# A 1024x1024 product as seven half-size products, and the order of tokens that goes with it

## The chip, the cores and the metric

The kernel runs on one core of a Trainium2 chip. The metric is the device time of one execution in microseconds. The kernel before takes 1306.87 us, the median of 3 runs (1304.11 to 1307.63). One execution of it was profiled, and its span from the first to the last instruction is 1304.7 us.

The names of the engines in the profile are PE (matrix products; PEld is its weight load), DVE and ACT (elementwise work), POOL (little elementwise work here) and SP (which only issues transfers here; the rows "SPq" are its queue).

## The reference

One layer of a hybrid network on 512 tokens of width 1024, in float32. A conditioning vector gives nine rows of modulation (`mod`), and three sublayers add to x:

```
mod = silu(c) @ w_ada + b_ada            # sh1, sc1, g1, sh2, sc2, g2, sh3, sc3, g3
u = rms_norm(x, ffn1_norm_g) * (1 + sc1) + sh1
x = x + 0.5 * g1 * swiglu(u, ffn1_w_in, ffn1_w_out)          # width 2816

u = rms_norm(x, mix_norm_g) * (1 + sc2) + sh2
z = u @ w_mix + b_mix                                        # q, k, v, gates of two branches
y_a = ... mLSTM in chunks of 64 ...;  y_b = ... forgetting attention, 16 heads ...
merged = sigmoid(g_a) * (y_a @ w_branch_a) + sigmoid(g_b) * (y_b @ w_branch_b)
x = x + g2 * (merged @ w_out)                                # 512x1024 @ 1024x1024

u = rms_norm(x, ffn2_norm_g) * (1 + sc3) + sh3
x = x + 0.5 * g3 * swiglu(u, ffn2_w_in, ffn2_w_out)
```

The change concerns the line with `w_out` and what stands around it: the branch products ahead of it, the norm and the first products of the second FFN behind it.

## The kernel before

**Products.** A 1024-deep product is cut into 8 blocks of 128 (`k`). Each float32 operand is held as two parts, high and low, and each matmul of the algorithm is three on PE (`mm3`, L139 to L143): high by high (L141), then one with a low part (L142), then the other (L143). The operand that is loaded into the array stands on the left of the comma in a profile row's inputs, the one that streams stands right. `split` makes the parts of a weight that a transfer has brought into a tile `raw`: ACT copies it into `wh` (L116), DVE subtracts into `wl` (L118). There are 3 buffers for `raw` and 4 each for `wh` and `wl`. Two groups of four accumulation banks exist, `g` and `t`. All weights come over SP's queue (L106).

**Branch stage** (`run`, L1670 to L1693). Eight products of branch a, which are called A0 to A7 here, then eight of branch b, B0 to B7. Each is 24 matmuls of 128x512 into one `g` bank, for 128 columns of the output and all 512 tokens (`branch`, L1416). Half way through a product the weights of the next are asked for. Each ends with the out step of DVE at L1430, (gate + 1) times the bank, which gives `ta` in branch a and `sg` in branch b. In branch b POOL adds the two branches' results (L1691), ACT takes the high part of the sum (`mh`, L1692) and DVE the low part (`ml`, L1693): that is `merged`, transposed, 128 columns to a tile. After each product `step` runs what is due of a chain of small work (`tick`) and one load of 512 KB of w_ada, which DVE accumulates into the modulation rows (L318, L320).

**The product with w_out** comes in two halves of its 1024 output columns. The first (`token_gemm`, L673) has a `t` bank for each block of 128 tokens; the weights come in four chunks of 256 rows, the first two for all blocks of tokens, the last two block by block, so that a finished block goes on at once: DVE scales the bank by a broadcast row (L796) and adds it to x (L798), ACT squares x with a sum (L243). The second half is in `passage` (L697), in `g` banks, block by block, and what follows is written out in a fixed order there (`pin`): the norm of the first 256 tokens (`xnorm`: the factor by a chain of small DVE instructions, L261 and L160 to L168, then `xn` at L267 on DVE and L268 on ACT), its transposes on PE (`norm_turn`, L294), the parts of u (`u_part`: L277, L279 on ACT, L283 on DVE), the same for the other 256 tokens, and the first four column groups of the second FFN's product (`first`, L771), 256 tokens at a time. `mod_cols` (L385) turns the modulation rows of the last norm into columns by a transpose on PE (L389) of what `mod_load` has fetched (L382) after a row was stored (L376).

**Order.** A scheduler places the instructions of an engine where they are not pinned, by its own costs; each engine then runs its instructions strictly in that order. The profile's rows name tiles without their numbers; the order lists give the numbers.

## Time and profile before

| | |
|---|---|
| time, median of 3 (lowest, highest) | 1306.87 us (1304.11, 1307.63) |
| span of the profiled execution | 1304.7 us |
| branch a, A0 to A7 with its last preparations | 819 to 863 us of the span |
| branch b, B0 to B7 | 863 to 906 us |
| w_out, norm, the first column groups of FFN2 | 906 to 978 us |
| PE busy | 1291.3 us |
| DVE, ACT, POOL busy | 961.2, 632.3, 34.6 us |

The profiled execution's own time is its span of 1304.7 us; what lies outside it is the 2.2 us up to the median of the runs. The page gives busy time of each engine, its share of the span, and the chain of work that ended last. A timeline row gives the start in the span, the duration, the engine, the line, the operation with output and inputs, and in brackets the idle time of that engine before it and what ended that. A window row gives, for a stretch of the span, the sum of busy time and for PE, PEld, DVE, ACT and POOL the busy time with the count of instructions, then the granted clock of PE, the share of the transfer engines, and GB/s.

### The profile page before, as it was taken

The numbers are of one execution on the slowest core, as the hardware profiler recorded it, in microseconds if no ns is written. First come the engines' busy times: TensorE is split into PE (matmuls) and PEld (weight loads), VectorE is DVE, ScalarE is ACT, GpSimd is POOL, SyncE is SP. The second block draws the span as 40 slices with busy tenths as digits, with TensorE's granted clock in tenths as the row PEclk, the third lists the DMA queues.
The fourth block names the chain that finished last, engine by engine and source line by source line (L and its number), as shares of the span: only waits on it lengthen the run. The fifth ranks groups of instructions, "written<-read, shape, count | busy, mean of one in ns | idle before, by whom it ended". The sixth has DMA issues, their size and how long they took to land.

```text
span 1304.7 us, 17739 instructions
## 1 busy us (share of the span) xinstructions
PE 1291.3 (99%) x6265; PEld 1085.2 (83%) x6265; DVE 961.2 (74%) x1740; ACT 632.3 (48%) x1040; POOL 34.6 (3%) x57
## 2 busy tenths in 40 slices
PE   8999999999999999999999999999999999999998
PEld 6788888888889888788888888888898888888887
DVE  6877777478789787999998776677566656635787
ACT  5633232355467655666574766234372223223741
POOL 1000000000010101000000000003000000000000
PEclk9999999999999999999999999999999999999999
DMA  9999978464865534545455583777539778634573
GB/s 294 276 328 303 316 266 292 139 185 155 296 187 144 173 89 130 178 133 155 138 128 149 130 151 102 230 256 242 186 114 321 257 233 278 219 97 136 167 272 143
DMA packets 245257, 260.48 MB, mean 200 GB/s; under 512 B 57312, under 2 KB 184960, under 8 KB 245168
## 3 DMA queue, kind: packets, MB, share of 16 engines
q1 hardware_dynamic: 240464, 251.41, 63.0%
q10 hardware_dynamic: 4384, 7.88, 2.0%
q8 instruction: 49, 0.80, 0.3%
q14 instruction: 40, 0.33, 0.1%
q0 software_dynamic: 320, 0.06, 0.0%
HBM read 220.43 MB, written 38.87 MB: 199 GB/s over the span
## 4 chain that ended last, share of the span: by engine, by line
PE 93%; DVE 4%; DMA 1%; ACT 1%; issue 1%; POOL 0%; ACTq 0%; DVEq 0%; POOLq 0%; SPq 0%
PE g L142 24%; PE g L141 24%; PE g L143 24%; PE t L141 4%; PE t L142 4%; PE t L143 4%; PE g L949 2%; PE t L1362 1%; PE t L1332 1%; PE t L1305 1%; PE t L949 1%; PE t L1306 1%; PE t L837 0%; DVE wl L118 0%; DMA h_d<-hn 0%
## 5 line engine op out<-in xcount | busy, mean ns | idle before, releaser
L116 ACT ACTIVATE wh<-raw 128x1024 fp32r<-128x1024 f32 (+2 forms) x246 | 248.9, 1016 | 348.8 <-PE g L142 109.9
L118 DVE TENSOR_TENSOR wl<-raw,wh 128x1024 fp32r<-128x1024 f32 (+2 forms) x246 | 288.1, 1175 | 155.0 <-ACT wh L116 131.0
L141 PE MATMUL g<-uh,wh 128*128 128x512 f32 (+1 forms) x880 | 340.9, 387 | 0.0
L143 PE MATMUL g<-uh,wl 128*128 128x512 f32 (+1 forms) x880 | 339.6, 386 | 0.0
L142 PE MATMUL g<-ul,wh 128*128 128x512 f32 (+1 forms) x880 | 339.1, 385 | 0.0
L143 PEld LDWEIGHTS g<-uh,wl 128*128 128x128 f32 x880 | 165.3, 188 | 33.6
L141 PEld LDWEIGHTS g<-uh,wh 128*128 128x128 f32 x880 | 165.4, 188 | 32.9 <-issue 0.6
L142 PEld LDWEIGHTS g<-ul,wh 128*128 128x128 f32 x880 | 165.4, 188 | 32.2
L141 PE MATMUL g<-wh,uh 128*128 128x512 f32 (+1 forms) x256 | 97.6, 381 | 0.0
L143 PE MATMUL g<-wh,ul 128*128 128x512 f32 (+1 forms) x256 | 96.6, 377 | 0.0
L142 PE MATMUL g<-wl,uh 128*128 128x512 f32 (+1 forms) x256 | 96.5, 377 | 0.0
L320 DVE SCALAR_TENSOR_TENSOR acc<-raw,ccol,acc 128x1024 f32<-128x1024 f32 (+1 forms) x56 | 56.7, 1032 | 40.1 <-DMA raw<-in_w_ada_dram 40.0
L141 PE MATMUL t<-wh,A 128*128 128x512 f32 x176 | 68.6, 390 | 0.0
L142 PE MATMUL t<-wl,A 128*128 128x512 f32 x176 | 68.6, 390 | 0.0
L143 PEld LDWEIGHTS g<-wh,ul 128*128 128x128 f32 x256 | 48.2, 188 | 8.9
L142 PEld LDWEIGHTS g<-wl,uh 128*128 128x128 f32 x256 | 48.3, 188 | 8.4
L141 PEld LDWEIGHTS g<-wh,uh 128*128 128x128 f32 x256 | 48.2, 188 | 8.2
L141 PE MATMUL g<-yh,wh 128*128 128x512 f32 x128 | 49.8, 389 | 0.0
L143 PE MATMUL g<-yh,wl 128*128 128x512 f32 x128 | 49.8, 389 | 0.0
L142 PE MATMUL g<-yl,wh 128*128 128x512 f32 x128 | 49.8, 389 | 0.0
L1316 ACT ACTIVATE S<-S,mn 128x128 f32<-128x128 f32 (+1 forms) x64 | 35.6, 557 | 26.2 <-DVE mn L1308 20.4
L460 ACT ACTIVATE A<-E 128x768 fp32r<-128x768 f32 x22 | 18.6, 846 | 52.6 <-DVE E L459 52.6
(370 smaller groups left out, 2230.3 us busy)
## 6 DMA issues: line engine op xcount, KB each, us to landing
raw<-in_ffn_w_in_dram SPq DMA_DIRECT2D x82, 512.0 KB, 4.9
raw<-in_w_ada_dram SPq DMA_DIRECT2D x48, 512.0 KB, 4.8
raw<-in_w_mix_dram SPq DMA_DIRECT2D x46, 512.0 KB, 4.3
sa<-in_ffn_w_out_dram SPq DMA_DIRECT2D x22, 512.0 KB, 5.4
sb<-in_ffn_w_out_dram SPq DMA_DIRECT2D x44, 256.0 KB, 5.7
ws<-sa SPq DMA_DIRECT2D x22, 512.0 KB, 4.8
ws<-sb SPq DMA_DIRECT2D x44, 256.0 KB, 3.8
raw<-ws SPq DMA_DIRECT2D x44, 256.0 KB, 3.6
```

The costliest lines, as they stand in the source:

```text
L116: nc.scalar.activation(hi, src, AF.Copy)
L118: self.last_lo = nc.vector.tensor_tensor(lo, src, hi, op=SUB)
L141: pin(mm(ps, lh, rh, start=start, stop=False))
L142: pin(mm(ps, lh, rl, start=False, stop=False))
L143: self.last_mm = pin(mm(ps, ll, rh, start=False, stop=stop))
L320: nc.vector.scalar_tensor_tensor(a, r[:, s], c, a, op0=MUL, op1=ADD)
L460: nc.scalar.activation(A1[:, 0:3, :], E[:, 0:3, :], AF.Copy)
L949: pin(nc.tensor.matmul(acc_ps[b], (wl if p == 1 else wh)[:, b % 2, s], self.ul[k] if p == 2 else self.uh[k], start=k == 0 and p == 0, stop ...
L1305: nc.tensor.matmul(ps[:, :w], q[:, s], k[:, :w], start=True, stop=False)
L1306: nc.tensor.matmul(ps[:, :w], q[:, s], kl[:, :w], start=False, stop=True)
L1316: nc.scalar.activation(S[:, ws], S[:, ws], AF.Exp, scale=-1.0, bias=m, accum_out=sm[:, qb:qb + 1])
L1332: tr = lambda b, c, qb, kb: nc.tensor.transpose(b[:, c:c + P], S[:, P_OFF[qb] + kb * P:P_OFF[qb] + (kb + 1) * P], self.ident)
```

## The change

**Seven products in place of eight.** With the 1024 columns of `merged` cut into even and odd blocks of 128 (A1 and A2, so E and Ra in the code) and the 512 tokens into the first and last 256, and w_out cut into even and odd row blocks and into two halves of its columns, the product is a 2x2 product of blocks, done by seven block products with sums on both sides (the form of Strassen's scheme with few additions). Each block product is 256 tokens by 512 rows by 512 columns: two banks, 24 matmuls of 128x512. Seven make 168 matmuls, where the kernel before has 192.

**Sums of weights** (`out_sums`). During branch a, after each product, one step of a generator loads a pair of row blocks of w_out (four transfers of 256 KB into tiles that u has left free), makes four sums by DVE subtractions (L689 to L692), held behind the low part of the weights that was made last, and stores them (four transfers of 256 KB) to scratch memory. Four pairs make 32 transfers.

**Sums of merged** (`merge_slot`, `merge_pair`). POOL's add writes into `mt`, which uses the tiles of x. After each second product of branch b, DVE and ACT make the seven left operands of that pair in high and low parts: eight DVE instructions of 128x256 or 128x512 and four of ACT. They take the place of L1692 and L1693. x is loaded later, behind the merges.

**The passage** is written anew. The products run in the order A11, A12, S2, S1, S4, S3, A22. A11, S2, S1 and S4 go one onto the other in the same two `t` banks; ACT copies the banks out after each of the first three (`p1`, `u2`, `u4`). A12 is in two `g` banks, S3 and A22 one onto the other in two more. `into` scales a result and adds it to x (L777, L779, L780). Tokens 0 to 255 are complete after S4: their norm runs then, and their transposes stand on PE behind S3. Tokens 256 to 511 are complete after A22. Parts, `first` and the second norm follow.

```diff
-    def mm3(self, ps, lh, ll, rh, rl, start, stop):
+    def mm3(self, ps, lh, ll, rh, rl, start, stop, on=False):
...
+    def out_sums(self, w):
+        nc = self.nc
+        V = nc.vector.tensor_tensor
+        self.wo = [self.dp.tile([P, NK // 2, 512], F32, name=self.nm("wo")) for _ in range(4)]
+        tags = [f"{a}{k}" for k in range(NK) for a in ("uh", "ul")]
+        ts = {}
+        def load(i):
+            ts[i] = [self.up.tile([P, 512], F32, name=self.nm("so"), tag=tags[5 * (i % 3) + n]) for n in range(5)]
+            with self.tc.issue_after(self.last_raw.ins):
+                for n, (r, h) in enumerate(((0, 0), (0, 1), (1, 0), (1, 1))):
+                    nc.sync.dma_start(ts[i][n], w[(2 * i + r) * P:(2 * i + r + 1) * P, h * 512:(h + 1) * 512])
+        def sums(i):
+            a, b, c, d, e = ts[i]
+            with self.tc.issue_after(self.last_lo.ins):
+                V(e, d, b, op=SUB)
+                V(b, b, a, op=SUB)
+                V(d, d, b, op=SUB)
+                V(c, c, d, op=SUB)
+        def store(i):
+            a, b, c, d, e = ts.pop(i)
+            for t, o in zip((b, e, c, d), self.wo):
+                nc.sync.dma_start(o[:, i, :], t)
...
+    def merge_pair(self, i, bp):
+        E, Ra, S, Rb = self.mt
...
+        nc.scalar.activation(A[:, 0, :], E[:, 0, :], AF.Copy)
+        V(A[:, 1, :], E[:, 0, :], A[:, 0, :], op=SUB)
+        nc.scalar.activation(Rah, Ra, AF.Copy)
+        V(Ral, Ra, Rah, op=SUB)
+        V(S[:, 0, :], E[:, 1, :], Ra[:, 1, :], op=ADD)
+        V(S[:, 1, :], S[:, 0, :], E[:, 0, :], op=SUB)
+        nc.scalar.activation(Sh, S, AF.Copy)
+        V(Sl, S, Sh, op=SUB)
+        V(Rb[:, 1, :], Ra[:, 0, :], S[:, 1, :], op=SUB)
+        V(Rb[:, 0, :], E[:, 0, :], E[:, 1, :], op=SUB)
+        nc.scalar.activation(Rbh, Rb, AF.Copy)
+        V(Rbl, Rb, Rbh, op=SUB)
...
-    def passage(self, lhs, w_out, w_in, bp, G, sh):
+    def passage(self, w_out, w_in, bp, gain):
...
+        weights("A11")
+        weights("A12")
...
+        for tb in range(2):
+            product("A11", Z, tb, True)
+            pin(nc.scalar.activation(p1[tb], Z[tb], AF.Copy))
...
+        weights("S2")
+        X = [self.gbank() for _ in range(2)]
+        product("A12", X, 0, True)
+        product("A12", X, 1, True)
...
+        t = into(0, 0, X[0], p1[0])
+        product("S2", Z, 0)
...
+        weights("S4")
+        product("S1", Z, 0)
...
+        m3 = self.mod_load(6)
+        weights("S3")
+        apart(2)
+        product("S4", Z, 0)
+        t = into(0, 1, Z[0])
+        self.x_sq(0, 1, t)
+        product("S4", Z, 1)
+        G, sh3 = self.mod_cols(6, gain, m3, self.tbank)
+        t = into(1, 1, Z[1])
+        self.x_sq(1, 1, t)
+        weights("A22")
+        V4 = [self.gbank() for _ in range(2)]
         xn = self.xnorm(0, bp)
...
+        product("S3", V4, 0, True)
...
         b = self.norm_turn(0, xn)
...
+        for tb in range(2):
+            product("A22", V4, tb)
+        for k in range(NK):
+            part(0, k)
...
             for m in range(NK):
                 ta.append(self.branch(m, 0, bp, yp.tile([P, T], F32, name=self.nm("ta"), tag="qk", bufs=16), sg[m] if m < 2 else None))
                 step()
+                next(pw, None)
...
-                nc.gpsimd.tensor_tensor(t, t, ta[m], op=ADD)
-                nc.scalar.activation(self.mh[m], t, AF.Copy)
-                nc.vector.tensor_tensor(self.ml[m], t, self.mh[m], op=SUB)
+                nc.gpsimd.tensor_tensor(self.merge_slot(m), t, ta[m], op=ADD)
+                if m % 2:
+                    self.merge_pair(m // 2, bp)
```

**What moves.** Three places on DVE. The first is branch a. `ta_8251`, `ta_8288` and `ta_8327` are the out steps of A1, A2 and A3 before, `wl_8346`, `wl_8385`, `wl_8424` and `wl_8463` the low parts of the weights of A4 to A7:

```order
L1430 SCALAR_TENSOR_TENSOR ta_8251<-sg_8101,g_8252 128x512
L118 TENSOR_TENSOR wl_8346<-raw_8343,wh_8345 128x1024
L320 SCALAR_TENSOR_TENSOR acc_8134<-raw_8362,ccol,acc_8134 128x512
L320 SCALAR_TENSOR_TENSOR acc_8135<-raw_8362,ccol,acc_8135 128x512
L118 TENSOR_TENSOR wl_8385<-raw_8382,wh_8384 128x1024
L1430 SCALAR_TENSOR_TENSOR ta_8288<-sg_8289,g_8291 128x512
```

In the changed kernel `ta_8298`, `ta_8354` and `ta_8410` are the out steps of A2, A3 and A4, `wl_8373` and `wl_8429` the low parts of A4 and A5:

```order
L1531 SCALAR_TENSOR_TENSOR ta_8298<-sg_8299,g_8301 128x512
L1531 SCALAR_TENSOR_TENSOR ta_8354<-sg_8355,g_8357 128x512
L118 TENSOR_TENSOR wl_8373<-raw_8370,wh_8372 128x1024
L320 SCALAR_TENSOR_TENSOR acc_8118<-raw_8389,ccol,acc_8118 128x512
L320 SCALAR_TENSOR_TENSOR acc_8119<-raw_8389,ccol,acc_8119 128x512
L689 TENSOR_TENSOR so_8345<-so_8344,so_8342 128x512
L690 TENSOR_TENSOR so_8342<-so_8342,so_8341 128x512
L691 TENSOR_TENSOR so_8344<-so_8344,so_8342 128x512
L692 TENSOR_TENSOR so_8343<-so_8343,so_8344 128x512
L1531 SCALAR_TENSOR_TENSOR ta_8410<-sg_8411,g_8413 128x512
L118 TENSOR_TENSOR wl_8429<-raw_8426,wh_8428 128x1024
```

Before, the low part of A4 stood ahead of the out step of A2; now it stands behind the out step of A3, the product just ahead of A4, and the same holds for A5 (behind A4), A6 and A7. On PE, A4 follows A3 so; its third matmul reads `wl_8373`:

```order
L143 MATMUL g_8357<-yh_8188,wl_8317 128x512
L141 MATMUL g_8413<-yh_8160,wh_8372 128x512
L142 MATMUL g_8413<-yl_8161,wh_8372 128x512
L143 MATMUL g_8413<-yh_8160,wl_8373 128x512
```

The first of these rows is A3's last matmul, and the others are A4's first three.

The second place is the end of branch b. Before, `sg_8861` is the out step of the last but one product, and the weights of the first w_out chunks follow with one low part of `merged` between them:

```order
L1430 SCALAR_TENSOR_TENSOR sg_8861<-sg_8861,g_8863 128x512
L118 TENSOR_TENSOR wl_8988<-raw_8985,wh_8987 128x1024
L1693 TENSOR_TENSOR ml_8099<-sg_8861,mh_8091 128x512
L118 TENSOR_TENSOR wl_8994<-raw_8991,wh_8993 128x1024
```

After, `sg_8976` is the out step of B7, `mt_8973` and `mt_8974` with `mr` and `mo` belong to the last pair's merge, `wl_9048` and `wl_9054` are the two halves of A12's weights:

```order
L1531 SCALAR_TENSOR_TENSOR sg_8976<-sg_8976,g_8978 128x512
L765 TENSOR_TENSOR wl_9048<-raw_9045,wh_9047 128x1024
L730 TENSOR_TENSOR mt_8973<-mt_8971,mt_8972 128x256
L729 TENSOR_TENSOR mr_9014<-mt_8972,mr_9013 128x512
L731 TENSOR_TENSOR mt_8973<-mt_8973,mt_8971 128x256
L734 TENSOR_TENSOR mt_8974<-mt_8972,mt_8973 128x256
L733 TENSOR_TENSOR mo_9012<-mt_8973,mo_9011 128x512
L737 TENSOR_TENSOR mr_9016<-mt_8974,mr_9015 128x512
L765 TENSOR_TENSOR wl_9054<-raw_9051,wh_9053 128x1024
```

The second half of A12's weights now stands behind the whole merge of the last pair, which cannot begin before B7 has ended.

The third place is the first norm. Before, the last rows ahead of its chain (L261, L160 and so on) are the low parts of a column group of FFN2 and one block's scale and add:

```order
L722 TENSOR_TENSOR fl_9168<-raw_9164,fh_9166 128x512
L722 TENSOR_TENSOR fl_9169<-raw_9164,fh_9167 128x512
L796 SCALAR_TENSOR_TENSOR rs_9196<-g_9079,gb_9076 128x512
L798 TENSOR_TENSOR x_8900<-x_8900,rs_9196 128x512
L261 SCALAR_TENSOR_TENSOR v_9218<-ss_8913 128x2
L160 TENSOR_SCALAR rq_9220<-v_9218 128x2
```

After, `t_9031` and `t_9032` are the banks after S4, and `wl_9321` and `wl_9327` the weights of A22:

```order
L793 TENSOR_TENSOR fl_9274<-raw_9270,fh_9272 128x512
L793 TENSOR_TENSOR fl_9275<-raw_9270,fh_9273 128x512
L779 SCALAR_TENSOR_TENSOR rs_9292<-t_9031,gb_9101 128x512
L779 SCALAR_TENSOR_TENSOR rs_9314<-t_9032,gb_9101 128x512
L780 TENSOR_TENSOR x_9058<-x_9058,rs_9292 128x512
L780 TENSOR_TENSOR x_9060<-x_9060,rs_9314 128x512
L765 TENSOR_TENSOR wl_9321<-raw_9318,wh_9320 128x1024
L765 TENSOR_TENSOR wl_9327<-raw_9324,wh_9326 128x1024
L261 SCALAR_TENSOR_TENSOR v_9332<-ss_9029 128x2
L160 TENSOR_SCALAR rq_9334<-v_9332 128x2
```

Two blocks of tokens end together now, and both halves of A22's low part stand between their adds and the chain of the norm.

More of the change, by code (lines that the diff above doesn't have):

```diff
@@ new lines, in passage, with part @@
+        b = self.norm_turn(0, xn)
+        x_spill((0, 1))
+        hi0, lo0 = whole(0)
+        hi3, lo3 = whole(3)
+        def part(hf, k):
+            self.u_part(hf, b, k, bp, G, sh3, True, V)()
+        for tb in range(2):
+            product("A22", V4, tb)
+        for k in range(NK):
+            part(0, k)
+            if k == 1:
+                hi0()
+            if k == 3:
+                lo0()
+        for tb in range(2):
+            into(tb + 2, 1, ts[tb])
+            self.x_sq(tb + 2, 1, ts[tb])
@@ L769, in passage @@
+        for tb in range(2):
+            t = into(tb + 2, 0, V4[tb])
+            self.x_sq(tb + 2, 0, t)
+        hi3()
         xn = self.xnorm(1, bp)
+        lo3()
         pp = [self.gbank() for _ in range(4)]
@@ L782, in passage @@
         for k in range(NK):
-            part(1, b, k, True)
+            part(1, k)
         first(1, (0, 1))
@@ L1670, in run @@
         with tc.tile_pool(name="br", bufs=1) as bp:
[L1671 to L1672 removed]
+            pw = self.out_sums(A["w_out"][0])
+            self.ma = {}
             def step():
```

202 lines of the change are left out of this document (102 added, 100 removed).

## The prediction

> **What bounds the kernel now.** I read the page first.
>
> ```profile
> span 1304.7 us, 17739 instructions
> PE 1291.3 (99%) x6265; PEld 1085.2 (83%) x6265; DVE 961.2 (74%) x1740; ACT 632.3 (48%) x1040; POOL 34.6 (3%) x57
> PE 93%; DVE 4%; DMA 1%; ACT 1%; issue 1%; POOL 0%; ACTq 0%; DVEq 0%; POOLq 0%; SPq 0%
> ```
>
> PE is busy 99% of the span and is 93% of the chain that ended last. So matmuls taken away are worth their full issue interval, and every wait that PE gains is paid in full. The windows of the three stages say the same of the place that changes, and how full DVE and the transfers are there:
>
> ```profile
> 819.00:863.00 44.00, 44.00 (x196) 36.44 (x195) 29.29 (x41) 15.86 (x21) 0.00 (x0) 1.00 0.79 238
> 863.00:906.00 43.00, 43.00 (x192) 35.34 (x191) 35.13 (x44) 15.51 (x20) 10.74 (x7) 1.00 0.83 270
> 906.00:978.00 72.00, 72.00 (x424) 63.43 (x423) 41.54 (x79) 39.23 (x72) 2.81 (x2) 1.00 0.48 151
> ```
>
> PE has no idle time in 159 us. DVE is busy 29.3 of 44 us in branch a, 35.1 of 43 in branch b, 41.5 of 72 behind them. Of the waits of PE, the groups of the whole span that lie here are two, together 2.1 us:
>
> ```profile
> PE t L372 <- DVE hl L367: 1.8, 1, 1.8
> PE t L294 <- DVE xn L267: 0.3, 1, 0.3
> ```
>
> The question is therefore not what an engine's total becomes, but whether the new orders make PE wait for more than the removed matmuls gave.
>
> **What is removed: 24 matmuls.** From PE's timeline across the end of A1 and the start of A2; the first and the last of these rows are eleven matmuls apart:
>
> ```profile
> 828.43 0.39 PE L141 MATMUL g<-yh,wh 128*128 128x512 f32 x1
> 829.56 0.39 PE L143 MATMUL g<-yh,wl 128*128 128x512 f32 x1
> 830.92 0.39 PE L143 MATMUL g<-yh,wl 128*128 128x512 f32 x1
> ```
>
> (830.92 − 828.43) / 11 = 0.226 us from one to the next, so 24 fewer are 5.4 us, and one block product, also 24, lasts 5.4 us. The w_out product has no stall that could swallow the gain, by the windows. **Gain 5.4.**
>
> **Term 1, branch a, four waits.** The row at 829.56 above is the last matmul of its product: DVE's out step follows it.
>
> ```profile
> 829.99 0.69 DVE L1430 SCALAR_TENSOR_TENSOR ta<-sg,g 128x512 f32<-128x512 f32 x1 [0.22 <-PE g L143]
> 833.22 1.22 DVE L118 TENSOR_TENSOR wl<-raw,wh 128x1024 fp32r<-128x1024 f32 x1 [2.54 <-ACT wh L116]
> 834.36 1.41 DVE L320 SCALAR_TENSOR_TENSOR acc<-raw,ccol,acc 128x512 f32<-128x512 f32 x2
> 857.19 0.69 DVE L1430 SCALAR_TENSOR_TENSOR ta<-sg,g 128x512 f32<-128x512 f32 x1 [1.88 <-PE g L143]
> 857.79 0.88 DVE L318 TENSOR_SCALAR acc<-raw,ccol 128x512 f32<-128x512 f32 x2
> ```
>
> Now the low part of the next product's weights stands behind the out step, for A4 to A7. With t the start of the last matmul: out step at t + 0.43 (829.99 − 829.56), the next DVE instruction 0.60 later (857.79 − 857.19), the low part takes 1.22: it is there at t + 2.25. The third matmul of the next product reads it and would start at t + 3 x 0.226 = t + 0.68. That is 1.57 us each, 6.3 for four. Nothing covers it: PE is in strict order and its next rows are of the same product. The low end is 6.0 (a low part at 1.14, its spacing to the next row, 834.36 − 833.22), the high end 6.3. This alone takes more than the gain.
>
> The sums' own work is hidden at first. Sixteen subtractions of about 0.6 us are 9.6 us in A0 to A6 on a DVE with 14.7 us free of 44. The transfers are nearer to a bound: 0.79 of 44 us is 34.8 us of busy time now, and 32 transfers of 256 KB are 8.4 MB, which at the best rates the trace shows
>
> ```profile
> 980.00:982.00 2.00, 2.00 (x11) 1.65 (x10) 0.47 (x2) 0.85 (x1) 0.00 (x0) 1.00 0.99 390
> 982.00:984.00 2.00, 2.00 (x11) 1.65 (x10) 1.50 (x3) 0.99 (x1) 0.00 (x0) 1.00 1.01 404
> ```
>
> take 21 us. Less four loads of x that now come later (1 MB, 2.6 us), that is 53 us of transfers in 44 + 6.3 = 50.3 us. Weights arrive ahead of their use: the low part made at 833.22 is for A4, and A2 starts with the matmul behind the row at 829.56, so A4 two products later, at 840.6. So 3 us can be late without a wait. I take 0, with 3 as the high end.
>
> **Term 2, branch b.** POOL's add gates each merge, and its duration swings:
>
> ```profile
> 882.76 1.29 POOL L1691 TENSOR_TENSOR sg<-sg,ta 128x512 f32<-128x512 f32 x1 [4.95 <-DVE sg L1430]
> 900.27 2.14 POOL L1691 TENSOR_TENSOR sg<-sg,ta 128x512 f32<-128x512 f32 x1 [3.57 <-DVE sg L1430]
> ```
>
> The low part of B3's weights now stands behind the first pair's merge, which waits for the add behind B1's out step. The operations of half width cost about 0.34 by this row and the next one, which starts 0.34 later:
>
> ```profile
> 978.57 0.42 DVE L458 TENSOR_TENSOR E<-E,Ra 128x256 f32<-128x256 f32 x1
> 978.91 1.22 DVE L118 TENSOR_TENSOR wl<-raw,wh 128x1024 fp32r<-128x1024 f32 x1
> ```
>
> Chain from B1's last matmul: 0.43 + 0.60 + add 2.14 + 0.34 + 0.34 + 0.60 + 0.34 + 0.60 + 0.60 + 1.22 = 7.2 us. B2 with three matmuls of B3 is 27 x 0.226 = 6.1. So 1.1, or 0.25 with the short add. I take 1.0; range 0.2 to 1.8, the top with other merges that meet a full DVE (35.1 us of 43, and eight instructions, 5 x 0.34 + 3 x 0.60 = 3.5 us, come for two of 0.60 in each pair).
>
> *The shared port.* The Trainium skill, "SBUF — State Buffer", section "Who interferes with whom", says that a VectorE operation with two inputs in SBUF and a GpSimd operation that reads SBUF exclude one another for the whole instruction. The two rows above, 1.29 and 2.14 for the same add, fit it; by that rule the merges, all of two SBUF inputs, would push the adds towards the long one, and term 2 goes to its 1.1.
>
> **Term 3, the second half of A12's weights.** It stands behind the last pair's merge. From B7's last matmul at t8, by the same prices: the add ends at 0.43 + 0.60 + 2.14 = 3.17, ACT's copy of 0.63 behind it at 3.80, then DVE's 0.60 + 0.34 + 0.34 + 0.60 + 0.60 and the low part's 1.22: t8 + 7.5, and 7.7 with a wait for the second copy. Its first reader is the eighth matmul of A12, 32 after t8: t8 + 7.2. That would be 0.4 if DVE were idle at t8. It is rather full: with 2.3 us more for each pair it has 44 us of work in 43, and one pair's merge, 3.5 to 4, can still stand ahead. I take the middle, 2.5; range 0.4 to 4.5.
>
> **Term 4, the modulation columns in S4.** The row is stored and read back before the transpose on PE:
>
> ```profile
> 919.20 0.26 SPq L376 DMA_DIRECT2D mod_d<-br  x1
> 922.63 0.38 SPq L382 DMA_DIRECT2D mr<-mod_d  x1
> DMA to landing us min/median/max: 3.6/3.6/3.6
> ```
>
> 3.4 + 3.6 = 7.0 us after the row is ready, which follows two small matmuls at A12's end. The transpose stands 36 matmuls, 8.2 us, later, and SP's queue is shared with w_in's loads. Behind it the low part of S4's weights waits for two scale-and-adds: about 1.2 by the same prices. Together 1.5; range 0 to 3.
>
> **Term 5, the first norm.** Before, 24 matmuls of the last block and a lead of a whole block covered it but for the 0.3 above. Rows of the chain:
>
> ```profile
> 944.42 0.63 ACT L243 ACTIVATE rs<-x 128x512 f32<-128x512 f32 x1 [3.35 <-DVE x L798]
> 945.18 0.16 DVE L261 SCALAR_TENSOR_TENSOR v<-ss 128x2 f32<-128x2 f32 x1 [0.85 <-ACT rs L243]
> 946.76 0.88 DVE L267 TENSOR_SCALAR xn<-x,rq 128x512 f32<-128x512 f32 x2
> ```
>
> Now, from the last matmul of S4 at e: 0.43, two DVE steps 1.20, the add 0.69, the square with its sum 0.76 to the start of L261; but ACT's copies of A22's weights wait for S4's end, since their buffers are S4's, and DVE's two low parts of them (1.22 + 1.14) stand ahead of L261. A copy is 1.02 by the page:
>
> ```profile
> L116 ACT ACTIVATE wh<-raw 128x1024 fp32r<-128x1024 f32 (+2 forms) x246 | 248.9, 1016 | 348.8 <-PE g L142 109.9
> ```
>
> Sum: 0.43 + 1.20 + 0.69 + 0.76 + 1.06 (a copy with its issue) + 1.22 + 1.14 + 1.58 (946.76 − 945.18) + 0.88 = 9.0. S3 covers 24 x 0.226 = 5.4, and 0.2 of start: 3.3 to 3.6. FFN2's column group, whose low parts stand ahead of all this, has a transfer of 512 KB to wait for, 4.9 us by the page's row:
>
> ```profile
> raw<-in_ffn_w_in_dram SPq DMA_DIRECT2D x82, 512.0 KB, 4.9
> ```
>
> So I take 4.0; range 3.0 to 5.5. If L261 didn't stand behind the two low parts, it would be 1.2.
>
> **Term 6, the second norm.** A22 ends; then four scale-and-adds on DVE behind the eight low parts of u, four squares and the chain. ACT's sixteen part rows at 0.45 each
>
> ```profile
> 949.81 0.56 ACT L277 ACTIVATE uh<-t,sh,G 128x256 fp32r<-128x256 f32 x1
> 950.26 0.56 ACT L279 ACTIVATE uf<-t,sh,G 128x256 f32<-128x256 f32 x1
> 975.41 0.28 PE L141 MATMUL g<-uh,wh 128*128 128x256 f32 x1
> 975.53 0.28 PE L142 MATMUL g<-ul,wh 128*128 128x256 f32 x1
> ```
>
> with a copy of weights are 8.3, the eight DVE steps of 0.60 behind them 4.8, the last square 0.8, the chain 1.6 and xn 0.9: 16.4 us from the transposes. A22 (5.4) and 72 matmuls of 256 columns at 0.12 (975.53 − 975.41; 8.6), with the wait for the first parts, are some 15.2. Take 1.2; range 0 to 2.5.
>
> **Sum.** 6.3 + 1.0 + 2.5 + 1.5 + 4.0 + 1.2 = 16.5 lost, 5.4 gained: +11.1. On the profiled execution 1304.7 + 11.1 = 1315.8; it lies 2.2 below the median of the runs, so 1318 against 1306.87. All low ends: 6.0 + 0.2 + 0.4 + 0 + 3.0 + 0 − 5.4 = +4.2, 1311. All high ends with the transfers: 6.3 + 3 + 1.8 + 4.5 + 3 + 5.5 + 2.5 − 5.4 = +21, 1328.
>
> **The rivals.** *A, the waits don't come about.* Decides: the low parts of A4 to A7 are made early enough after all, because the out steps are not what they wait for at run time, and the passage is covered as before. The point is a wait under 5.4 / 4 = 1.36 us per product in branch a with nothing behind it. For it: PE never waited at 819 to 978 before. Against it: DVE is in strict order, and 1.57 is a sum of three rows. Time: with all six terms at nothing 1301.5, faster.
>
> *B, only branch a stalls.* While PE waits 6.3 us there, ACT, the transfers and DVE run on, and the later chains find their covers. For it: DVE is only 41.5 of 72 us busy behind the branches. Against it: terms 3 and 5 are chains from the end of a product, and no lead shortens these. Time: 1306.87 + 6.3 − 5.4 + 0.5 = 1308.
>
> *C, transfers bound branch a.* 53 us of them in 50, and if the lead is gone, A5 to A7 wait for raw weights, and DVE, which then waits for `so` tiles ahead of the out steps, holds the out steps too. Price: the 3 us over and another 4 for order. For it: 0.79 of the engines' time is in use already. Against: the lead of one product. Time: 1318 + 7 = 1325.
>
> *D, the waits are long enough to slow PE's clock.* After the first wait of the kernel, 6 us, matmuls of one size take 0.208 each, and 0.12 later:
>
> ```profile
> PE t L212 <- DMA rowsC<-in_b_ada_dram: 6.0, 1, 6.0
> ...
> 6.18 6.24 PE L837 MATMUL t<-ident 128*128 128x128 f32 x30
> 12.26 1.95 PE L853 MATMUL t<-ccol,ar 128*128 128x128 f32 x16
> ```
>
> If terms 3 and 5 are near their high ends, 4.5 and 5.5 (3.5 over the sum), and do the same, each costs up to 6.24 − 30 x 0.122 = 2.6 us more: 1318 + 3.5 + 5.2 = 1327. For it: these rows. Against it: the granted clock of the windows above is 1.00 throughout, and no row of a mid-span wait shows a slower matmul. The Trainium skill, "TensorE: Matmul & The Clock Gate", section "Part 1: The HAM clock gate", says that the clock falls to half after an idle window of about 3.4 us and comes back after as long of work. By that rule term 5 at 4.0 would pay it and term 3 at 2.5 not.
>
> That the change doesn't do what it says isn't a rival: the product rows on PE are 24 fewer.
>
> **How the numbers follow.** Forecast, the sum with its terms within their ranges: 0.62. A 0.08, B 0.15, C 0.07, D 0.08. The likeliest is the sum, 1318; its own range is 1311 to 1328. With B the range to give reaches down to 1307; A and the ends of C stay outside: 1307 to 1328. What a measurement here can tell from no change is about 0.3%, 3.9 us. Faster is A, 0.08. Within 0.3%, 1303 to 1310.8, is B without its upper part, 0.13, and a little of the forecast's low end, 0.02. Slower is the rest, 0.77.
>
> **What would show it.** In the profile after: waits of PE for `wl` at L118 (or its line in the passage), four of 1.6 us in branch a, each behind an out step of DVE; if they are absent or under 1.36, term 1 is wrong and A nearer. One wait for `wl` at L765 seven matmuls into A12 (term 3), and one at the transposes, L294, for `xn` of about 4 us (term 5). The w_out products should take 168 x 0.226 = 38 us of PE time. Waits for `wh` or `raw` in branch a would speak for C, a granted clock under 1.00 after 880 us for D. The forecast is wrong if the waits of PE behind 819 us sum to under 9 us.

## The result, and the profile after

The changed kernel takes 1338.56 us, the median of 4 runs (1334.32 to 1339.58), where the kernel before took 1305.76 beside it. The ratio is 1.0243, with an interval of 1.0223 to 1.0264: 32 us slower, outside the range of 1307 to 1328. The profiled execution's span is 1337.0 us, 32.3 over the one before, and it is that difference which is divided up here.

The page of the changed kernel, its first rows and the chain that ended last:

```profile
span 1337.0 us, 17823 instructions
PE 1298.4 (97%) x6241; PEld 1085.2 (81%) x6241; DVE 995.1 (74%) x1794; ACT 643.7 (48%) x1060; POOL 37.0 (3%) x57
PE 79%; DVE 9%; DMA 6%; ACT 2%; issue 2%; SPq 1%; POOL 0%; POOLq 0%; ACTq 0%; DVEq 0%
```

PE runs 24 fewer instructions and is busy 7 us longer, so some of its matmuls have become slower. Its share of the chain fell from 93% to 79%, and the share of transfers (DMA) rose from 1% to 6%. The waits of PE by group, those of a microsecond or more, but for the kernel's opening one. A row gives the engine and bank, the line that waited, what ended the wait, then the total in us, how often, and the longest:

```profile
PE g L143 <- DVE wl L118: 6.7, 6, 2.0
PE t L294 <- DVE xn L267: 6.2, 3, 5.3
...
PE g L141 <- ACT wh L116: 4.7, 2, 3.8
PE t L142 <- DVE wl L765: 4.5, 2, 3.5
PE g L142 <- DVE wl L765: 3.4, 1, 3.4
PE t L141 <- ACT u L840: 1.0, 1, 1.0
```

Where the stages begin and end is read from the first and last matmul with `yh`, the last out step with `ta`, and the first matmul of FFN2 that has 512 columns. Before:

```profile
L141 PE MATMUL g<-yh,wh x128: 389/389/398, 818.9 to 905.8; 128*128 128x512 f32 x128
...
L1430 DVE SCALAR_TENSOR_TENSOR ta<-sg,g x8: 677/680/690, 825.3 to 862.9; 128x512 f32<-128x512 f32 x8
...
977.57 0.40 PE L141 MATMUL g<-uh,wh 128*128 128x512 f32 x1
```

and after:

```profile
L141 PE MATMUL g<-yh,wh x128: 388/389/629, 817.7 to 922.0; 128*128 128x512 f32 x128
...
L1531 DVE SCALAR_TENSOR_TENSOR ta<-sg,g x8: 675/687/691, 824.5 to 873.6; 128x512 f32<-128x512 f32 x8
...
1009.70 0.40 PE L141 MATMUL g<-uh,wh 128*128 128x512 f32 x1
```

Branch a lasted 44.0 us and lasts 55.9; branch b, up to two matmuls (0.6 us) after the last of these `yh` rows, 43.5 and 49.0; the rest up to FFN2's full-width matmuls 71.2 and 87.1. So the loss is 11.9, 5.5 and 15.9 us, the last with the 5.4 of the removed matmuls already in it; the stage starts 1.2 earlier, and what follows is as long as before. Gross that is 38.7 us of loss against a forecast of 16.5. Windows of the changed kernel, which do not follow the stages exactly, since these now end at 873.6, 922.6 and 1009.7:

```profile
819.00:865.00 46.00, 38.73 (x159) 30.26 (x158) 28.03 (x39) 7.46 (x8) 0.00 (x0) 0.96 1.01 330
865.00:913.00 48.00, 43.85 (x182) 34.45 (x181) 40.79 (x59) 17.02 (x26) 10.05 (x5) 0.96 0.66 197
913.00:989.00 76.00, 61.69 (x273) 49.83 (x272) 57.03 (x90) 40.27 (x68) 5.50 (x4) 0.91 0.63 200
```

Three things stand in them: a transfer share of 1.01 in branch a (0.96 over its whole 55.9 us), where it had been 0.79; idle time of PE in all three; and a granted clock under 1.00 in all three, where it had been 1.00.

### The profile page after: what moved, and what is told of

It reads as the page before. It is cut to its first block, busy times and chain, and to the rows that moved or that the text cites. A ratio compares the mean times of both kernels' runs of the same rounds, so it can differ in the third digit from the quotient of the medians.

```text
span 1337.0 us, 17823 instructions
## 1 busy us (share of the span) xinstructions
PE 1298.4 (97%) x6241; PEld 1085.2 (81%) x6241; DVE 995.1 (74%) x1794; ACT 643.7 (48%) x1060; POOL 37.0 (3%) x57
## 4 chain that ended last, share of the span: by engine, by line
PE 79%; DVE 9%; DMA 6%; ACT 2%; issue 2%; SPq 1%; POOL 0%; POOLq 0%; ACTq 0%; DVEq 0%
PE g L143 20%; PE g L142 20%; PE g L141 20%; PE t L141 3%; PE t L142 3%; PE t L143 3%; PE t L1463 1%; PE g L1050 1%; PE t L1433 1%; DVE wl L118 1%; DMA raw<-in_w_branch_a_dram 1%; PE t L1406 1%; PE t L1407 1%; ACT wh L116 1%; PE t L1050 1%
## 5 line engine op out<-in xcount | busy, mean ns | idle before, releaser
L116 ACT ACTIVATE wh<-raw 128x1024 fp32r<-128x1024 f32 (+2 forms) x238 | 240.6, 1015 | 354.8 <-PE g L142 129.9
L118 DVE TENSOR_TENSOR wl<-raw,wh 128x1024 fp32r<-128x1024 f32 (+2 forms) x238 | 276.9, 1167 | 138.0 <-ACT wh L116 118.5
L142 PEld LDWEIGHTS g<-ul,wh 128*128 128x128 f32 x880 | 165.5, 188 | 32.3
```

The lines of the kernel that those rows point to most:

```text
L116: nc.scalar.activation(hi, src, AF.Copy)
L118: self.last_lo = nc.vector.tensor_tensor(lo, src, hi, op=SUB)
L142: pin(mm(ps, lh, rl, start=False, stop=False, skip_group_check=on))
```

## Branch a: order or bytes

Theory one was the forecast's: the low parts of A4 to A7 stand behind the out steps on DVE. Theory two is the rival C: the transfers of the sums fill the stage. Rows of the changed kernel from SP, ACT, PE and DVE around A5 and A6:

```profile
836.85 4.12 SPq L684 DMA_DIRECT2D so<-in_w_out_dram  x4
...
842.52 0.38 SPq L106 DMA_DIRECT2D raw<-in_w_branch_a_dram  x1
...
849.79 1.06 ACT L116 ACTIVATE wh<-raw 128x1024 fp32r<-128x1024 f32 x1 [9.28 <-DMA raw<-in_w_branch_a_dram]
...
850.90 0.50 PE L141 MATMUL g<-yh,wh 128*128 128x512 f32 x1 [3.75 <-ACT wh L116]
...
859.78 1.22 DVE L118 TENSOR_TENSOR wl<-raw,wh 128x1024 fp32r<-128x1024 f32 x1
...
861.05 0.50 PE L143 MATMUL g<-yh,wl 128*128 128x512 f32 x1 [1.52 <-DVE wl L118]
```

The wait at 861.05 is theory one's: 1.52 us idle, 1.7 from start to start, for a price of 1.57. But such a wait stands only in A6 and A7. Ahead of A5 PE waits 3.75 us for a weight tile whose transfer was issued at 842.5 and landed 7 us later, and that is theory two's. Six runs divide the two.

**Only the order put right.** In branch a the out step is held behind the next low part:

```diff
-        nc.vector.scalar_tensor_tensor(dst, sg, 1.0, ps, op0=ADD, op1=MUL)
+        with self.tc.issue_after(self.last_lo.ins) if i == 0 else nullcontext():
+            nc.vector.scalar_tensor_tensor(dst, sg, 1.0, ps, op0=ADD, op1=MUL)
```

> The changed kernel with one thing different: in branch a the out step of a product is held behind the low part of the next product's weights on DVE, so that no low part waits for an out step. Theory one (the order on DVE is what branch a loses, four waits of 1.6 us): about 6 us come back, 1332 us, and PE's waits for wl in branch a are gone. Theory two (the 32 transfers of the sums fill branch a, and the weights come late whatever the order): at most 3 us come back, 1336 to 1339 us, and PE's waits for wl turn into waits for wh behind transfers of raw.

It took 1334.95 us (ratio to before 1.0232, 1.0211 to 1.0252), an interval that overlaps the changed kernel's: by the medians 3.6 us came back, by the ratios 1.4, so that a gain isn't clear of the noise. The waits of A6 and A7 are gone; the one for `wh` stays as it was, as the groups of this run show (the row with `wl` is A4's and B3's):

```profile
PE g L141 <- ACT wh L116: 4.0, 2, 3.8
...
PE g L143 <- DVE wl L118: 2.1, 2, 1.6
```

Branch a, measured as above, still lasted 52.7 us in this run's profile, 8.7 more than before. The time lies between the two theories' forecasts; the waits that are left are theory two's.

**No sums at all.**

```diff
-               "S1": sum_w(T1), "S3": sum_w(T3), "A22": sum_w(T4), "S2": sum_w(T2)}
+               "S1": raw_w(0, 1), "S3": raw_w(0, 0), "A22": raw_w(1, 0), "S2": raw_w(1, 1)}
...
-            pw = self.out_sums(A["w_out"][0])
...
-                next(pw, None)
```

> The changed kernel without the sums of w_out: no loads, subtractions or stores in branch a, and the four block products that took a sum take a plain block of w_out (so the product with w_out isn't computed rightly). Both theories: branch a lasts 43.5 us again in place of 55.5, and the rest stays as it is, 1326 us. If the late transfers also feed the waits behind branch a, the later stages shorten too, to 1318. What stays over 1305.8 + 5.4 - 5.4 is the price of the merges and the passage alone.

1320.3 us (1.0119; 1.0099 to 1.0139). Both branches are as long as before, branch b with all its merges:

```profile
L141 PE MATMUL g<-yh,wh x128: 389/389/397, 818.5 to 905.4; 128*128 128x512 f32 x128
```

86.9 us from the first to the last of these, like the 86.9 before. So the 17.4 us of the two branches are not there without the sums of weights, and the passage alone costs 15 us more than it did. The time came out near the 1318 that stood for late transfers that carry on into the later stages.

**The sums alone, and their bytes.** Two runs put the sums into the kernel before, unused. The second makes them an eighth as wide:

```diff
-                    nc.sync.dma_start(ts[i][n], w[(2 * i + r) * P:(2 * i + r + 1) * P, h * 512:(h + 1) * 512])
+                    nc.sync.dma_start(ts[i][n][:, 0:64], w[(2 * i + r) * P:(2 * i + r + 1) * P, h * 512:h * 512 + 64])
...
-            a, b, c, d, e = ts[i]
+            a, b, c, d, e = [x[:, 0:64] for x in ts[i]]
...
-                nc.sync.dma_start(o[:, i, :], t)
+                nc.sync.dma_start(o[:, i, 0:64], t[:, 0:64])
```

> The kernel before, with the sums of w_out made and stored in branch a as in the changed kernel, and not used. It prices the sums with the old passage behind them. If branch a's loss is its own and is not made worse by what follows: 12 us over before, 1318 us. If only the order on DVE costs: 6.3, 1312 us. If the old passage takes part of it back, because its own transfers and low parts are ahead by then: less.

> The kernel before with the sums in branch a as in the run that only adds them (1316.1 us), but every one of the 32 transfers and 16 subtractions covers 64 columns in place of 512: the same count in the same places of SP's queue, an eighth of the bytes. If the bytes are what branch a loses: 1305 to 1307 us. If the places in SP's queue are (each group of four ahead of the next weights): 1312 to 1316 us. DVE's order comes out a little better here, the low part ahead of the out step for A4, A6 and A7, so up to 3 us less than 1316 say nothing on either.

The sums alone: 1316.11 us (1.0089; 1.0071 to 1.0106), 12 us over before; its branch a loses 11 us and its branch b, which has no merges of pairs, 1. Thin: 1305.46 us (1.0014; 1.0002 to 1.0025). The window of branch a, first of the sums alone, then thin:

```profile
819.00:863.00 44.00, 37.49 (x154) 29.23 (x153) 27.41 (x37) 7.51 (x8) 0.00 (x0) 0.96 0.99 337
```

```profile
819.00:863.00 44.00, 43.12 (x189) 34.96 (x188) 29.18 (x51) 14.62 (x20) 0.00 (x0) 1.00 0.79 240
```

The same 32 issues stand in SP's queue in both, and with an eighth of the bytes they cost some 3 us at most. So the bytes bind: in the first window the transfer engines are at 0.99 with 337 GB/s. The subtractions are an eighth as wide too, but the wait ahead of A5 ended on ACT's copy, which had waited for a transfer and not for DVE, and DVE was busy only 27.4 of 44 us with the full sums. In the thin run most low parts also stand ahead of the out steps, since smaller sums changed the scheduler's order, and this run alone doesn't clear the order. The next two do their part.

**The order alone, no sums.**

```diff
+                if 3 <= n < NK - 1:
+                    sh = [P, NK, P]
+                    r = self.raw(sh, [(lambda t: t, A["w_branch_a"][0][:, (n + 1) * P:(n + 2) * P].rearrange("(k p) n -> p k n", p=P))])
+                    self.w_next = [self.wp.tile(sh, F32R, name=self.nm(s), tag=s, bufs=4) for s in ("wh", "wl")]
+                    nc.scalar.activation(self.w_next[0], r, AF.Copy)
+                    self.w_late = r
...
+        if self.w_late is not None and 3 <= n < NK - 1:
+            with self.tc.issue_after(last.ins):
+                self.last_lo = nc.vector.tensor_tensor(self.w_next[1], self.w_late, self.w_next[0], op=SUB)
```

> As the run without the sums, and in branch a the low parts of A4 to A7 are put behind the out steps of A3 to A6 on DVE, as they stand in the changed kernel. It prices the order alone, with no transfer of the sums beside it. Theory one: 6.3 us over the run without the sums, four waits of PE of 1.6 us start to start. If a clock drop is behind much of branch a's loss, it would not show here, since each wait is under 2 us.

1332.1 us (1.0214; 1.0197 to 1.0231), 12 over the run without sums, where 6.3 was expected. The group of waits for `wl`, then the two matmuls of PE around the longest wait, then the SP row of the transfer that it ended on:

```profile
PE g L143 <- DVE wl L1540: 5.4, 3, 1.9
```

```profile
841.53 0.39 PE L142 MATMUL g<-yl,wh 128*128 128x512 f32 x1
844.98 0.79 PE L141 MATMUL g<-yh,wh 128*128 128x512 f32 x1 [3.06 <-ACT wh L1532]
```

```profile
840.07 0.38 SPq L106 DMA_DIRECT2D raw<-in_w_branch_a_dram  x1
```

Three waits for `wl` of 1.5 to 1.9 are the forecast's. The fourth is another: this edit also moved PE's order. The first two matmuls of A5 and of A6 now stand ahead of A4's third, as the order of PE has it (the numbers tell the tiles apart; the trace has the same lines from 840.85 to 846.00):

```
L141 MATMUL g_8353<-yh_8160,wh_8329 128x512
L142 MATMUL g_8353<-yl_8161,wh_8329 128x512
L141 MATMUL g_8392<-yh_8160,wh_8368 128x512
L142 MATMUL g_8392<-yl_8161,wh_8368 128x512
L141 MATMUL g_8431<-yh_8160,wh_8407 128x512
L142 MATMUL g_8431<-yl_8161,wh_8407 128x512
L143 MATMUL g_8353<-yh_8160,wl_8330 128x512
```

So at 844.98 PE waits in A4 for A6's weights. These were asked for at 840.07, where the run without sums asks at 835.11: there are three `raw` buffers, and one whose low part is made late comes free late. The clock is at half for 6.8 us from 844.10, near the end of that wait. The run shows that waits of the forecast's size come when a low part stands behind the out step, three where four were expected; the order's whole price it doesn't show, since the mixed rows on PE are its own and not the changed kernel's. In the changed kernel the order put right gave back 1.4 to 3.6 us; nearly all of branch a's 12 came back only where the bytes were gone.

**The sums on another queue.** The same sums in the kernel before, their transfers issued by POOL.

```diff
-                    nc.sync.dma_start(ts[i][n], w[(2 * i + r) * P:(2 * i + r + 1) * P, h * 512:(h + 1) * 512])
+                    nc.gpsimd.dma_start(ts[i][n], w[(2 * i + r) * P:(2 * i + r + 1) * P, h * 512:(h + 1) * 512])
...
-                nc.sync.dma_start(o[:, i, :], t)
+                nc.gpsimd.dma_start(o[:, i, :], t)
```

> The kernel before with the same sums at full size, their 32 transfers issued on POOL's queue in place of SP's, so that no weights stand behind them; the low parts stand well ahead of the out steps again on DVE. If the bytes bind (53 us of transfers in 44): branch a still loses most, 1313 to 1316 us, with waits for wh behind raw. If SP's queue and DVE's order bind: 1305 to 1308 us.

1321.25 us (1.0127; 1.0112 to 1.0142), 5 us more than on SP's queue. Low parts stood ahead of the out steps here, and branch a still waits 4.2 us for `wh` and, at its end, 4.5 for `yh`. That agrees with theory two. Why POOL's queue is worse than SP's was not looked into.

## Behind the branches: two places in DVE's order

The wait that the forecast did not have stands in A11. Rows of the changed kernel from PE, DVE and POOL:

```profile
929.18 0.50 PE L142 MATMUL t<-wl,mo 128*128 128x512 f32 x1 [3.52 <-DVE wl L765]
...
926.84 2.29 DVE L765 TENSOR_TENSOR wl<-raw,wh 128x1024 fp32r<-128x1024 f32 x1
...
926.47 1.58 POOL L1793 TENSOR_TENSOR mt<-sg,ta 128x512 f32<-128x512 f32 x1 [7.93 <-DVE sg L1531]
```

The second half of A11's weights is made on DVE behind the third pair's merge and B6's out step, and DVE comes there late. It also takes 2.29 us in place of 1.22: POOL's add runs from 926.47 to 928.05, and the low part ends 1.08 after it. The Trainium skill, "SBUF — State Buffer", section "Who interferes with whom", says that a DVE operation with two inputs in SBUF and a GpSimd (POOL) operation that reads SBUF exclude one another; these rows agree, though one pair of rows doesn't show it to be the cause.

The second place is the first norm. Rows of DVE and PE:

```profile
966.11 1.28 DVE L779 SCALAR_TENSOR_TENSOR rs<-t,gb 128x512 f32<-128x512 f32 x2
...
970.40 2.36 DVE L765 TENSOR_TENSOR wl<-raw,wh 128x1024 fp32r<-128x1024 f32 x2 [1.81 <-ACT wh L764]
972.67 0.15 DVE L261 SCALAR_TENSOR_TENSOR v<-ss 128x2 f32<-128x2 f32 x1
...
974.25 0.88 DVE L267 TENSOR_SCALAR xn<-x,rq 128x512 f32<-128x512 f32 x2
...
974.79 3.86 PE L294 MATMUL t<-ident,xn 128*128 128x128 f32 x16 [5.34 <-DVE xn L267]
```

The chain is as forecast, with the two low parts of A22 just ahead of L261. The next runs all leave the sums of weights out, as above, so that the passage stands alone: 1320.3 us, with waits of 4.9 in A11, 2.0 in A12 and 5.0 at the transposes. A11's:

```profile
PE t L142 <- DVE wl L763: 4.9, 1, 4.9
```

**The add on DVE.**

```diff
-                nc.gpsimd.tensor_tensor(self.merge_slot(m), t, ta[m], op=ADD)
+                nc.vector.tensor_tensor(self.merge_slot(m), t, ta[m], op=ADD)
```

> As the run without the sums (1320.3 us), and the add of the two branches ahead of each merge is on DVE in place of POOL. Theory M (DVE runs 8 to 10 us late at the end of branch b because each merge waits on a round trip over POOL, and the low parts of A11's and A12's weights are queued behind that): the waits in A11 and A12, 4.9 and 2.0 us, fall under 2 and 1 us, the slow-clock stretches after them go, and about 8 us come back: 1312 us. Theory F (DVE is simply full there): eight adds of 0.6 us more make it later, the waits stay or grow: 1320 to 1325 us.

1315.66 us (1.0075; 1.0053 to 1.0096). The wait in A11 is gone and that in A12 is 2.2:

```profile
PE g L142 <- DVE wl L763: 2.2, 1, 2.2
```

So theory M holds for the first and not for the second, and of the 8 us expected 4.6 came by the medians, 5.7 by the ratios: A12's second half stands behind the last pair's merge wherever the add is made. In its place a new wait of 1.6 came for the modulation row (`mr`, L389), which the earlier delay had covered.

**A22's low parts behind xn.** In the passage `weights("A22")` makes only the high parts, and the subtractions follow the norm.

```diff
-        weights("A22")
+        lows = weights("A22", True)
...
+        for f in lows:
+            f()
```

> As the run without the sums, and the two low parts of A22's weights stand behind the first norm's xn on DVE instead of ahead of its chain. Theory N (those two stand in the norm's way): the wait at the transposes falls from 5.0 to about 2.6 us, and the slow stretch behind it goes or shortens: 1316 to 1318 us. If the chain waits for something else (the square, ACT's copies), it stays at 5.0 and 1320 us.

1315.92 us (1.0078; 1.0058 to 1.0097); the wait at the transposes fell from 5.0 to 1.8:

```profile
PE t L294 <- DVE xn L267: 2.8, 3, 1.8
```

Theory N holds. Not all of the gain is the norm's: A12's wait fell from 2.0 to 0.9 too, though the edit doesn't touch it, and no slow stretch stood behind it, so that the transposes began 4.2 us earlier after the branches, 3.1 of them by their own wait. A new wait of 1.0 for `rs` came right behind them.

**Both of these edits together.**

> As the run without the sums, with the add on DVE and A22's low parts behind the norm, both. If the two waits are separate: the sum of the two single gains, about 1308 to 1310 us by theories M and N. If the first stage's gain lets the norm begin earlier and changes nothing in its chain, the same sum; if less, the waits share a cause.

1309.33 us (1.0035; 1.0024 to 1.0046): by the ratios 5.7 and 5.4 us alone, 11.0 together (the bare medians give 4.6, 4.4 and 11.0, but the kernel before took 1303.71 beside the run without sums and 1305.49 beside these three). The two add, so they are separate.

**The rest of the passage in order.** The last pair's sums moved behind A12's low parts, the second column group's parts behind the norm, A22's low parts behind the two adds after it.

```diff
+        with tc.issue_after(self.low_last.ins):
+            self.merge_rest()
...
-        apart(2)
+        parts2 = apart(2, True)
...
+        for f in lows:
+            f()
...
+        parts2()
         hi0, lo0 = whole(0)
```

> As the run without the sums (so the product isn't computed rightly), with the passage put in order: adds on DVE; the last pair's sums, all but its Ra parts, behind the low parts of A12; the second column group's parts of FFN2 behind the first norm and A22's low parts behind the two adds after it. Theory M and N together (each wait of the passage is a place in DVE's order, not lack of time): the waits of 2.2, 1.9 and 1.0 us that were left go, with the slow stretch, some 7 us under the run with both changes: 1302 us, faster than before. If the chains themselves are too long for five products: 1306 to 1309 us.

1315.39 us (1.0078; 1.0063 to 1.0093): 6 us worse than the run with both, where 7 better was expected. Its groups:

```profile
PE t L294 <- DVE xn L267: 2.5, 3, 1.9
PE g L143 <- DVE wl L811: 2.5, 1, 2.5
PE t L141 <- ACT u L844: 2.1, 1, 2.1
...
PE g L142 <- DVE wl L768: 0.9, 1, 0.9
```

A12's wait fell from 2.2 to 0.9, and the first norm's from 1.9 to 0.2, as meant (the 1.9 left in that row is the second norm's). But the second group's `raw` is now held until 950, the next load of FFN2 waits for its buffer (issued at 949.5, where the run with both had one at 943.3), and ACT waits 2.3 us in the middle of the parts of u: a new wait of 2.5 for that weight and 1.9 at the second norm. The 2.1 for `u`, absent in the run with both, is another: ACT's copy of a bank stands behind copies of weights that waited 3.2 and 1.1 us for transfers of w_out. The theory that each wait is only a place in an order falls here; waits removed were paid for by later loads.

**The whole change with all of it.** The last run has the sums of weights, the edit of branch a's order from the first run, and the edits of the passage just shown.

> The changed kernel, with the sums, the out steps of branch a behind the next low part, and the passage in the order of the run before this. If the parts add: 1338.6 - 3.6 - (1320.3 - what the passage alone gives, about 1302) = 1317 us. If late transfers of branch a also hold the passage back: 1320 to 1325 us.

1329.31 us (1.0192; 1.0175 to 1.0209), 9 under the changed kernel and 25 over before. That is what the single results add to: 1338.6 − 3.6 − (1320.3 − 1315.4) = 1330.1. The forecast of 1317 had the passage alone at 1302.

## The clock

**Work that keeps PE busy.** 20 matmuls that nobody reads stand in the first norm's wait.

```diff
+        fb = self.gbank()
+        for _ in range(20):
+            pin(nc.tensor.matmul(fb, self.ma["S3"][0][0][:, 0:P], ops["S3"][0][0][:, 0, :], start=True, stop=True))
         b = self.norm_turn(0, xn)
```

> As the run without the sums, and 20 matmuls that compute nothing used stand between S3 and the transposes of the first norm, 4.5 us of the 5.0 that PE waits there. Theory C (a long wait makes PE's clock run at half for a stretch behind it): no slow stretch behind that wait in the records of the clock, and from the first transpose to the first matmul of FFN2's column groups 7.4 us in place of 9.2: 1318.5 us. If the transposes are slow for another reason: no change, 1320.3 us, or a little slower if the filler delays them.

The transposes, first without the filler and then with it:

```profile
957.58 3.86 PE L294 MATMUL t<-ident,xn 128*128 128x128 f32 x16 [4.97 <-DVE xn L267]
...
966.78 0.28 PE L141 MATMUL g<-uh,wh 128*128 128x256 f32 x1
```

```profile
957.51 2.25 PE L294 MATMUL t<-ident,xn 128*128 128x128 f32 x16 [0.62 <-DVE xn L267]
...
965.08 0.28 PE L141 MATMUL g<-uh,wh 128*128 128x256 f32 x1
```

16 transposes take 2.25 us in place of 3.86, and the stretch up to FFN2's first matmul 7.6 in place of 9.2: theory C. The kernel's time stayed at 1321.27 us (1.0116; 1.0095 to 1.0136), because the second norm's wait grew from 0.5 to 1.8 us. What the clock gave back there, the next chain took.

How long a wait must be is read from windows of 3.41 us laid on the clock's own steps. Of the changed kernel:

```profile
889.99:893.40 3.41, 1.42 (x7) 0.88 (x6) 3.41 (x7) 2.21 (x3) 0.00 (x0) 1.00 0.52 152
893.40:896.82 3.42, 3.42 (x9) 2.64 (x9) 3.42 (x6) 0.00 (x0) 2.34 (x1) 0.50 0.52 153
924.12:927.53 3.41, 1.54 (x6) 0.93 (x6) 3.35 (x6) 1.61 (x3) 1.06 (x1) 1.00 0.87 280
927.53:930.95 3.42, 1.77 (x8) 1.45 (x9) 3.38 (x5) 1.36 (x2) 0.51 (x1) 1.00 0.69 205
```

In the first, PE is idle for 1.99 us, and the second runs at 0.50. The wait of 3.52 us in A11 falls on two windows, 1.87 and 1.65 idle, and no slow one follows. Over the profiles of all runs with slow stretches, 30 such windows had 1.94 us or more without work on PE, four of them already at half clock, and a slow one followed each. At full clock three more had 1.89 to 1.93, followed by a slow one twice, and after 1.88 or less none was slow. Behind a slow window the next was slow too where it had 0.52 us or more without work, and not where it had 0.36 or less. A slow stretch of the changed kernel is 3.4 or 6.8 us long, and there are four. From 939.0 matmuls start 0.43 apart:

```profile
938.40 0.80 PE L142 MATMUL g<-wl,mr 128*128 128x512 f32 x1 [3.45 <-DVE wl L765]
939.00 0.63 PE L143 MATMUL g<-wh,mr 128*128 128x512 f32 x1
939.42 0.63 PE L141 MATMUL g<-wh,mr 128*128 128x512 f32 x1
```

Half of what PE worked in the four is 1.7 + 1.7 + 3.1 + 2.0 = 8.5 us.

## Why the prediction was wrong

The direction and the gain were right, the size was not: +32 where +11 was forecast. Of the gross loss of 38.7 us in the profiled run, 26 are idle time of PE in 14 waits, 8.5 the slow clock, and the rest, 4, is the 0.3 us that each wait costs beyond its idle time (0.16 up to the slot that the matmul ahead leaves, and a first interval of 0.34 in place of 0.23). One reading of the profile before was wrong as well, and no term rests on it: the two waits that the prediction puts in these stages, 2.1 us together, stood at 530.8 and 387.2 us, so there PE had no wait at all.

- **Term 1 (6.3; measured 11.9).** The step that failed is its second half: "3 us can be late without a wait. I take 0". The lead of two products was read from the kernel before, in an order where weights are asked for early. In the changed kernel SP's queue has the sums' groups ahead of them, and it stands still while earlier transfers land: of the 4.12 us of the four loads at 836.85 each is issued in 0.33 to 0.45, and the rest are gaps of up to 1.4. The 53 us of transfers in 50 that the term worked out were right (0.96 of 55.9 is 53.7), and that left no lead. Idle time is 8.7 of the 11.9, half a slow stretch 1.7, the rest what each wait costs beyond it. The thin run shows that the bytes decide. The order's own price was right for each wait (1.52 and 1.46 idle), and only two of the four came, since in A4 and A5 the weights were later still.
- **Term 2 (1.0; measured 5.5, with 1.7 of clock).** The wait in B3 came at 2.0, and one of 0.7 in B6 beside it. Without the sums of weights branch b lost nothing at all, and with the sums but without the merges of pairs 1 us: neither alone costs this, only the merges behind a branch a that ends late. By which path the lateness carries on wasn't tested.
- **Term 3 (2.5; measured 3.45 in A12, and 1.0 and 3.5 in A11).** A12's is the forecast's mechanism, inside its range of 0.4 to 4.5. What failed is the reading that only A12's second half stands behind a merge: A11's stands behind the pair before, in the same lists of DVE's order, and a DVE that waits for POOL and ACT in each merge comes there late though it isn't full.
- **Term 4 (1.5; measured 1.0).** Right in size; what PE waited for at S4 was ACT's copy of the bank (`u`, L840) and not the modulation row, whose wait came only once the stage ahead was shorter.
- **Term 5 (4.0; measured 5.3).** The mechanism was right, and the run with A22's low parts moved shows it; the size was inside the range of 3.0 to 5.5.
- **Term 6 (1.2; measured 0.4).** Covered at first. It returned at 1.8 with the filler and at 1.9 with the passage in order, but stayed at 0.5 in the two runs that only moved A22's low parts.
- **The rivals.** A and B did not come. C and D were both true, beside the forecast and not in its place, and the error of the range is there: they had 0.07 and 0.08 as alternatives, and each was priced from the forecast as if the other did not hold. The slow clock stood at nothing in the sum, and it measured 8.5. D's condition was too strict as well. It asked for waits near 4.5 and 5.5, and 2.0 us were enough in B3. The Trainium skill, "TensorE: Matmul & The Clock Gate", section "Part 1: The HAM clock gate", has the half clock and free-running windows of 3413 ns, and both agree with the records here; that a whole idle window is needed does not, since 1.94 us of 3.41 were always enough.

The 5.4 us are there in every run, but the best passage measured, which leaves out the sums that the product needs, is 1309.33 us and still over before.

## What to carry to other kernels

In a kernel that PE bounds, 24 matmuls fewer are worth 5.4 us only if nothing makes PE wait, and a wait of 2 us costs up to half of a 3.4 us stretch more than its length. Add the bytes of a change to the transfers of the very stage that carries them before giving weights a lead, and let the forecast's terms and the rivals that can hold together add up. When a stall is removed, look for the buffer that its instruction holds: a low part made later also held back the next load.

## What was not expected of the hardware

In these runs the clock fell from full to half on a fixed grid of 3.41 us by the idle time in one window (1.94 us and more always, 1.88 and less never), so a wait of 3.52 us that lay across two windows cost nothing extra and one of 1.99 inside one window cost 1.7 us. Transposes on PE follow it too (2.25 and 3.86 us for 16). Four loads on SP's queue took 4.12 us at 836.85 and 1.77 just ahead of branch a:

```profile
813.14 1.77 SPq L684 DMA_DIRECT2D so<-in_w_out_dram  x4
```

Full transfer engines alone don't explain it: their share was 1.00 from 813 to 818 too. What differs is gaps in the queue, of up to 1.4 us, that by the profile ended when earlier transfers of weights landed; in the thin run the same group took 3.44. The same bytes from POOL's queue made the kernel 5 us slower than from SP's.
